# Two experts of a mixture share the weight stream block by block

## The chip, the cores and the metric

The kernel runs on one core of one Trainium2 chip. The metric is the device time of one execution in microseconds. All matrix products are made in fp32 split in two: a weight w is turned into a rounded part (fp32r) and a remainder, and products are formed from the parts.

## What is computed

Two transformer layers over 256 tokens of width 1024. Each has a mixer (retention, latent attention and an mLSTM side by side), a layer norm, a feed-forward part and a second layer norm. The feed-forward part of layer 0 is dense, that of layer 1 is a mixture of eight experts. Only this last part is touched:

```python
logits = (t @ router).astype(jnp.float32)
top_v, top_i = lax.top_k(logits, 2)
top_w = jax.nn.softmax(top_v, axis=-1)
gate = jnp.sum(jax.nn.one_hot(top_i, 8) * top_w[..., None], axis=1)
for e in range(8):
    y = y + gate[:, e:e + 1] * ((silu(t @ wg[e]) * (t @ wu[e])) @ wd[e])
```

The matrices wg[e] and wu[e] are 1024x3584 and wd[e] is 3584x1024. With 256 tokens and two experts for each token, an expert gets 64 tokens on average. In these inputs experts 0, 1, 3 and 6 get at most 64 tokens, and experts 2, 4, 5 and 7 get more.

## The kernel before

The experts are worked in pairs, in the order `ORDER = [(0, 1), (2, 3), (4, 5), (6, 7)]`, and within a pair one expert is finished before the other begins. An expert has seven blocks of 512 hidden columns. `UNITS` lists the 56 blocks in their order. In a block TensorE makes three products from six weight pieces of 1 MB (128x2048 fp32): "gate" (two pieces, `half_mm`), "up" (two pieces, `half_mm`) and "down" (two pieces, `down`). The down product belongs to the block before: its hidden values must first be activated, multiplied, transposed and split. So a block's order on TensorE is gate of this block, up of this block, down of the previous block.

Each piece passes through four engines. SyncE issues its load into a "raw" place. ScalarE copies it as fp32r (the high part, L356) and VectorE subtracts that from the original (the low part, L357); both parts go to a pair of split places (`next_whole`). TensorE then uses the pair and so frees it. There are three pairs of split places and eleven raw places (four of `ring`, five of "e1r", two of "eb", taken in turn by `WHERE`), and three places more that are used once at the start. ScalarE and VectorE work in program order. `feed.conv` says how many half pieces ahead of TensorE's use a split is written into that order: with 4, the split of the second next piece is placed when a piece is begun.

TensorE has two ways of making a product, and a branch on the expert's token count chooses (`products`). With more than 64 tokens it makes three passes, high by high, low by high and high by low (L387 to L389), so 12 matmuls of 512 columns for a piece. With at most 64 tokens, the high parts of the tokens fill one half of the array and the low parts the other, so that two passes do (L1579, 8 matmuls for a piece), and the upper half of the result is added to the lower by one more matmul (L1603, `fold_in`), for which ScalarE copies the upper half out (L1600, `lower`). I call the two kinds three-pass and two-pass blocks.

`turn` transposes a block's hidden values (L1627 in three-pass blocks, L1633 in two-pass blocks, where there are eight small transposes in place of four) and splits them (ScalarE L397, VectorE L398, tile hT); down needs both. Where the next block belongs to the same expert, the transposes are put into the branch of the first quarter of up. Otherwise they have a branch of their own ahead of up. Likewise the fold of up's result stands inside a branch of down where the neighbour is of the same expert. Otherwise `folded` makes a branch of its own, and its three-pass side holds a small matmul of 8 columns (L1611) that only closes the accumulation. `hidden` is the Silu on ScalarE (L1615) and `hidden_times` the product of gate and up on VectorE (L1618).

The rest of the work hangs between the blocks as tasks, and `little()` advances the first of them by one step: `gather` (one-hot matmuls that collect the tokens of the next pair's experts, L1509, L1514, L1515, eight steps), `scatter` (scaling of a finished expert's sum, L1683 and L1684, and the matmuls that bring a pair's results back to the tokens, L1690 and L1715) and `way_back` (L1531 to L1537). Before the first counts are known (`fullest`), blocks run three passes without a branch. An expert's sum `z` takes two of the eight PSUM banks for as long as the expert runs; gate, up, the transposes and the tasks take the others in turn.

The loop body that the change edits:

```python
pg, low_g = half_mm(e)
little()
...
pu, low_u = half_mm(e, {0: split_hidden, 1: lambda: lower(pg, low_g)},
                    first, {3: [lambda: fold_in(pg, low_g)]} if low_g is not None else {})
little()
```

In `half_mm` and `down`, the dictionaries say what is written into the program after which of a product's four quarters.

Of the kernel before, what the change touches and what calls it, by code (L numbers as in the profile page):

```python
# [32 lines left out]
PIECE = 2048  # L33
NRING = 4
T1, T2, M2 = 6, 5, 2
# [25 lines left out]
FDN = 7  # L61
WHERE = [None] * 4 + ["e1r"] * 5 + ["eb"] * NEB
ONCE = ["xg0", "xg1", "xp"]
XG = ["xg%d" % i for i in (0, 1, 2, 3, 0, 1, 2, 3)]
CAP = 128
# [4 lines left out]
NS = D_FE // 512  # L70
ORDER = [(0, 1), (2, 3), (4, 5), (6, 7)]
UNITS = [(e, s) for pair in ORDER for e in pair for s in range(NS)]
LATS = [{
# [198 lines left out]
def tile_hybrid_block(  # L272
# [13 lines left out]

    ring = enter(name="ring", bufs=NRING)
    whl = enter(name="whl", bufs=MHL)
# [24 lines left out]
    def piece(src, a, b, by_col=False, pair=None, raw=None, cut=None, fine=False, at_once=False):  # L313


        if raw == "big":
            w = big([PIECE], F32)
        else:
            pl, n = raw or (ring, NRING)
            tag, n = (n, 1) if isinstance(n, str) else ("w", n)  # L320
            w = pl.tile([P, PIECE], F32, tag=tag, bufs=n, name="w")
        wv = w[:, :a * b].rearrange("p (a b) -> p a b", a=a)
# [42 lines left out]
    pairs = list(range(MHL))  # L365

    def next_whole():

        two = pairs[:2]
        pairs[:] = pairs[2:] + two  # L370
        return [whl.tile([P, PIECE], F32R, tag="wp%d" % i, bufs=1, name="wp") for i in two]

# [145 lines left out]
    def mixer(l, mq, ml, tabs, then):  # L518
# [77 lines left out]
        if l == 0:  # L596

            xv2 = x_t.rearrange("(k p) n -> p k n", p=P)
            xr = ring.tile([P, PIECE], F32, tag="w", name="xr").rearrange("p (k n) -> p k n", k=KT)
# [655 lines left out]
    def moe_weights():  # L1255
# [10 lines left out]
        def add(src, a, b):  # L1266
# [6 lines left out]
            else:  # L1273
                feed.add(lambda: piece(src, a, b, at_once=True, fine=fine))

# [8 lines left out]
        def quarters(w):  # L1284

            t = ring.tile([P, PIECE], F32, tag="w", bufs=NRING, name="w")
            tv = t.rearrange("p (k h n) -> p k h n", k=2, h=2)
# [135 lines left out]
    def moe(mp, free_order):  # L1423
# [159 lines left out]

        def half_mm(e, after={}, first=((), ()), few={}):
            xg = state[e][0]
            ps = bank()
            for k in range(0, KT, 2):
                if k % 4 == 0:
                    pcs = feed.next()
                m = pcs[k % 4 // 2]  # L1590
                products(e, [(ps, xg[:, k + i], [q[:, i] for q in m], k + i == 0, k + i == KT - 1) for i in range(2)],
                         first if k == 0 else ((), ()), few.get(k // 2, ()))
                soon_one()
# [26 lines left out]
        def turn(e, s, joined=False):  # L1620
# [19 lines left out]
            if last:  # L1640
                hT = mp.tile([P, 4, 2, P], F32R, tag=XG[5], name="hl")
            else:
# [106 lines left out]
        inner.enter_context(tc.manual_schedule(engines={mybir.EngineType.Activation, mybir.EngineType.DVE}))  # L1749
        feed.conv = 4  # L1750
        for i_, (e, s) in [(i // (2 * NS), u) for i, u in enumerate(UNITS)]:
            if s == 0:
                soon_all()
            end = (e, s) == UNITS[-1]
            pg, low_g = half_mm(e)
            little()
            split_hidden, first = lambda: None, ((), ())
            if prev and prev[0] == e and e in many:
                split_hidden, first = turn(*prev, True)
            elif prev:  # L1760
                split_hidden = turn(*prev)
            pu, low_u = half_mm(e, {0: split_hidden, 1: lambda: lower(pg, low_g)},
                                first, {3: [lambda: fold_in(pg, low_g)]} if low_g is not None else {})
            little()
            if prev:
                same = prev[0] == e and low_u is not None and not end

                def product():
                    if not same:
                        folded(e, pu, low_u)  # L1770
                    hidden(e, s, pg)
                    if end:
                        hidden_times(e, s, pu)

                down(*prev, {0: lambda: lower(pu, low_u), 1 if end else 2: product,
                             3: (lambda: turn(e, s)()) if end else lambda: hidden_times(e, s, pu)},
                     {2: [lambda: fold_in(pu, low_u)]} if same else {})
# [5 lines left out]
            else:  # L1783
                lower(pu, low_u)
                folded(e, pu, low_u)
                hidden(e, s, pg)
                hidden_times(e, s, pu)
            if s == 3 and e == ORDER[i_][0] and i_ + 1 < len(ORDER):
                tasks.append(gather(ORDER[i_ + 1]))
# [19 lines left out]
        with tc.If(v > CAP):  # L1809
            for e in range(NE):  # L1810
# [16 lines left out]
                with tc.For_i(0, D_FE, P) as f0:  # L1827
                    wg_ = ring.tile([P, PIECE], F32, tag="w", name="wgx")
                    wu_ = ring.tile([P, PIECE], F32, tag="w", name="wux")
                    wd_ = ring.tile([P, PIECE], F32, tag="w", name="wdx")  # L1830
                    wgv = wg_[:, :D].rearrange("p (k f) -> p k f", k=KT)
# [126 lines left out]
```

## Time and profile before

| what | value |
|---|---|
| time, median of three runs | 1393.18 us (1392.72 to 1393.56) |
| time of the profiled execution | 1393.02 us |
| span of the profiled execution | 1391.2 us |
| granted TensorE clock, mean | 0.994 of full speed |
| TensorE matmul busy | 1344.7 us, 97% |
| VectorE busy | 1195.2 us, 86% |
| ScalarE busy | 1004.8 us, 72% |
| first Silu of the experts | at 474.51 us |
| 56th and last Silu of the experts | at 1361.89 us |

The busy shares are averages over stages with different limits, so the table does not say what sets the pace of the experts. A matmul's end is modelled in this profile, so that a busy TensorE can still lose time: what it loses is read from the weight loads, which follow each other at an even pace when nothing is waited for.

### The profile page before, as it was taken

The numbers are of one execution on the slowest core, as the hardware profiler recorded it, in microseconds if no ns is written. First come the engines' busy times: TensorE is split into PE (matmuls) and PEld (weight loads), VectorE is DVE, ScalarE is ACT, GpSimd is POOL, SyncE is SP. The second block draws the span as 40 slices with busy tenths as digits, with TensorE's granted clock in tenths as the row PEclk, the third lists the DMA queues.
The fourth block names the chain that finished last, engine by engine and source line by source line (L and its number), as shares of the span: only waits on it lengthen the run. The fifth ranks groups of instructions, "written<-read, shape, count | busy, mean of one in ns | idle before, by whom it ended". The sixth has DMA issues, their size and how long they took to land. (4 is left out here: it accounts for less than half of the span.)

```text
span 1391.2 us, 19646 instructions
## 1 busy us (share of the span) xinstructions
PE 1344.7 (97%) x7021; PEld 1094.9 (79%) x7021; DVE 1195.2 (86%) x1358; ACT 1004.8 (72%) x1057; POOL 41.8 (3%) x66
## 2 busy tenths in 40 slices
PE   9999999999999999999999999999999999999995
PEld 8887999998888867666788866688888887667884
DVE  7998735468878899999988899988889889999895
ACT  6743534435733699999877899878788888988883
POOL 1021000001021000000000000000000000000000
PEclk9999999999999999999999999999999999999998
DMA  9373835663147989999999999999999999999961
GB/s 346 118 238 130 274 121 182 212 210 123 60 184 298 334 321 405 403 401 406 406 395 364 359 383 403 405 406 395 352 366 362 383 377 361 405 402 404 405 242 51
DMA packets 200036, 431.11 MB, mean 310 GB/s; under 512 B 9824, under 2 KB 44000, under 8 KB 199904
## 3 DMA queue, kind: packets, MB, share of 16 engines
q1 hardware_dynamic: 195952, 425.01, 82.4%
q0 software_dynamic: 864, 3.15, 0.6%
q8 instruction: 92, 1.51, 0.4%
q10 hardware_dynamic: 3088, 1.11, 0.4%
q14 instruction: 40, 0.33, 0.1%
HBM read 428.19 MB, written 1.05 MB: 309 GB/s over the span
## 5 line engine op out<-in xcount | busy, mean ns | idle before, releaser
L357 DVE TENSOR_TENSOR wp<-w,wp 128x2048 fp32r<-128x2048 f32 (+3 forms) x382 | 734.6, 1944 | 116.4 <-ACT wp L356 113.6
L356 ACT CAST wp<-w 128x2048 fp32r<-128x2048 f32 (+3 forms) x382 | 618.4, 1632 | 170.8 <-PE pm L389 48.3
L1579 PE MATMUL pm<-wp,xg 128*128 128x512 f32 x848 | 218.5, 404 | 3.8 <-DVE wp L357 1.7
L1579 PEld LDWEIGHTS pm<-wp,xg 128*128 128x128 f32 x848 | 153.0, 189 | 55.2 <-DVE wp L357 23.1
L387 PE MATMUL pm<-wp,xg 128*128 128x512 f32 x472 | 186.8, 396 | 0.0
L388 PE MATMUL pm<-wp,xg 128*128 128x512 f32 x472 | 184.4, 391 | 0.6 <-DVE wp L357 0.5
L389 PE MATMUL pm<-wp,xg 128*128 128x512 f32 x472 | 184.2, 390 | 0.0
L357 DVE TENSOR_TENSOR wp<-big,wp 128x2048 fp32r<-128x2048 f32 (+1 forms) x66 | 136.9, 2093 | 9.9 <-ACT wp L356 9.1
L1579 PE MATMUL z<-wp,hT 128*128 128x512 f32 x448 | 117.2, 403 | 17.8 <-DVE hT L398 15.6
L356 ACT CAST wp<-big 128x2048 fp32r<-128x2048 f32 (+1 forms) x66 | 115.0, 1757 | 13.7 <-PE pm L389 10.0
L1579 PEld LDWEIGHTS z<-wp,hT 128*128 128x128 f32 x448 | 80.0, 188 | 44.7 <-issue 25.9
L388 PEld LDWEIGHTS pm<-wp,xg 128*128 128x128 f32 x472 | 88.7, 188 | 19.6 <-DVE wp L357 2.2
L389 PEld LDWEIGHTS pm<-wp,xg 128*128 128x128 f32 x472 | 88.6, 188 | 18.8
L387 PEld LDWEIGHTS pm<-wp,xg 128*128 128x128 f32 x472 | 88.7, 188 | 17.8
L392 PE MATMUL pm<-big,wp 128*128 128x256 f32 x320 | 90.6, 283 | 0.0
L394 PE MATMUL pm<-big,wp 128*128 128x256 f32 x320 | 90.6, 283 | 0.0
L393 PE MATMUL pm<-big,wp 128*128 128x256 f32 x320 | 90.5, 283 | 0.0
L387 PE MATMUL z<-wp,hT 128*128 128x512 f32 x216 | 85.0, 393 | 0.0
L389 PE MATMUL z<-wp,hT 128*128 128x512 f32 x216 | 84.3, 390 | 0.2
L388 PE MATMUL z<-wp,hT 128*128 128x512 f32 x216 | 84.2, 390 | 0.0
L531 PE MATMUL pm<-wp,big 128*128 128x512 f32 (+1 forms) x288 | 69.5, 389 | 0.6 <-ACT big L397 0.2
L1600 ACT CAST low<-pm 64x512 fp32r<-64x512 f32 x109 | 63.5, 583 | 2.7
(325 smaller groups left out, 1818.5 us busy)
## 6 DMA issues: line engine op xcount, KB each, us to landing
w<-in_moe_w_up_dram SPq DMA_DIRECT2D x93, 1024.0 KB, 9.1
w<-in_moe_w_gate_dram SPq DMA_DIRECT2D x89, 1024.0 KB, 8.1
w<-in_moe_w_down_dram SPq DMA_DIRECT2D x88, 1024.0 KB, 8.8
big<-in_moe_w_gate_dram SPq DMA_DIRECT2D x21, 1024.0 KB, 10.1
big<-in_moe_w_down_dram SPq DMA_DIRECT2D x20, 1024.0 KB, 7.7
big<-in_moe_w_up_dram SPq DMA_DIRECT2D x17, 1024.0 KB, 8.0
w<-in_w_in_dram SPq DMA_DIRECT2D x16, 1024.0 KB, 7.7
w<-in_ffn_w_gate_dram SPq DMA_DIRECT2D x11, 1024.0 KB, 5.8
```

Source lines behind the costliest of these rows:

```text
L356: act.copy(hv[c], src_[c])
L357: dve.tensor_tensor(lv[c], src_[c], hv[c].bitcast(F32), op=OP.subtract)
L387: pe.matmul(ps, s[0], m[0], start=first, stop=False)
L388: pe.matmul(ps, s[0], m[1], start=False, stop=False)
L389: pe.matmul(ps, s[1], m[0], start=False, stop=last)
L392: pe.matmul(ps, s[0], m[0], start=first, stop=False)
L393: pe.matmul(ps, s[1], m[0], start=False, stop=False)
L394: pe.matmul(ps, s[0], m[1], start=False, stop=last)
L531: pe.matmul(o, s, m, start=start, stop=stop)
L1579: pe.matmul(ps, both, m[part], start=begin and part == 0, stop=last and part == 1)
L1600: act.copy(low[0][HALF:], ps[HALF:])
```

## The change

`ORDER` pairs expert 0 with 4, 1 with 5, 2 with 6 and 3 with 7, and `UNITS` runs the pair's blocks alternately: block 0 of expert 0, block 0 of expert 4, block 1 of expert 0, and so on. Every pair then has one two-pass and one three-pass expert. As two experts are open at a time, their sums hold four PSUM banks.

Two of the four `ring` places stay raw places, and when the experts' pieces begin the other two become a fourth pair of split places. Raw places are then nine (`MRING, 2`), and twelve pieces instead of fourteen can be loaded in advance. `feed.conv` goes from 4 to 5, so that the split of the third next piece is placed in the middle of a piece.

The transposes of the previous block's hidden values now stand ahead of the last quarter of gate, and their split behind gate. As two blocks in a row are never of one expert, they always have a branch of their own, and the fold of up's result is always made by `folded`, with L1611 on the three-pass side. The copy `lower` of up's result moves from behind down's first quarter to behind its second, and `hidden_times` from behind down's fourth quarter to behind its third. The first block is followed by one more `little()`, so that the token counts are loaded ahead of the second block. The tags of the gathered tokens (`XG`) follow the new pairs.

```diff
-NRING = 4
+NRING, MRING = 4, 2
...
-WHERE = [None] * 4 + ["e1r"] * 5 + ["eb"] * NEB
+WHERE = [None] * MRING + ["e1r"] * 5 + ["eb"] * NEB
...
-XG = ["xg%d" % i for i in (0, 1, 2, 3, 0, 1, 2, 3)]
+XG = ["xg%d" % i for i in (0, 2, 0, 2, 1, 3, 1, 3)]
...
-ORDER = [(0, 1), (2, 3), (4, 5), (6, 7)]
-UNITS = [(e, s) for pair in ORDER for e in pair for s in range(NS)]
+ORDER = [(0, 4), (1, 5), (2, 6), (3, 7)]
+UNITS = [(e, s) for pair in ORDER for s in range(NS) for e in pair]
...
+    wholes = []
+
     def next_whole():
-
-        two = pairs[:2]
-        pairs[:] = pairs[2:] + two
-        return [whl.tile([P, PIECE], F32R, tag="wp%d" % i, bufs=1, name="wp") for i in two]
+        if not wholes:
+            wholes[:] = [[(whl, "wp%d" % i) for i in pairs[j:j + 2]] for j in range(0, MHL, 2)] + [[(ring, n) for n in routes["free"]]]
+        wholes.append(wholes.pop(0))
+        return [pl.tile([P, PIECE], F32R, tag=n, bufs=1, name="wp") for pl, n in wholes[-1]]
...
-        feed.conv = 4
+        feed.conv = 5
...
-            pg, low_g = half_mm(e)
+            turned, first, before = [], {}, {}
+            if prev and prev[0] == e:
+                split, first[3] = turn(*prev, True)
+                turned.append(split)
+            elif prev:
+                before[3] = lambda: turned.append(turn(*prev))
+            pg, low_g = half_mm(e, {3: lambda: turned[0]() if turned else None}, first, {}, before)
             little()
-            split_hidden, first = lambda: None, ((), ())
-            if prev and prev[0] == e and e in many:
-                split_hidden, first = turn(*prev, True)
-            elif prev:
-                split_hidden = turn(*prev)
-            pu, low_u = half_mm(e, {0: split_hidden, 1: lambda: lower(pg, low_g)},
-                                first, {3: [lambda: fold_in(pg, low_g)]} if low_g is not None else {})
+            pu, low_u = half_mm(e, {1: lambda: lower(pg, low_g)}, {},
+                                {3: [lambda: fold_in(pg, low_g)]} if low_g is not None else {})
...
-                    if end:
-                        hidden_times(e, s, pu)
-
-                down(*prev, {0: lambda: lower(pu, low_u), 1 if end else 2: product,
-                             3: (lambda: turn(e, s)()) if end else lambda: hidden_times(e, s, pu)},
+                    hidden_times(e, s, pu)
+
+                down(*prev, {0 if end else 1: lambda: lower(pu, low_u), 1 if end else 2: product,
+                             3: (lambda: turn(e, s)()) if end else lambda: None},
                      {2: [lambda: fold_in(pu, low_u)]} if same else {})
...
                 hidden_times(e, s, pu)
+                little()
```

## Rows read from the trace of the kernel before

**Rows 1.** Windows: busy time of each engine in stretches of experts 2, 3, 5, 6

```profile
core 0: us, PE busy (x) PEld busy (x) DVE busy (x) ACT busy (x) POOL busy (x), PEclk, DMA share, GB/s
...
686.00:796.00 110.00, 110.00 (x519) 91.90 (x518) 96.50 (x67) 86.21 (x73) 0.00 (x0) 1.00 1.02 376
...
811.00:898.00 87.00, 80.93 (x351) 56.45 (x350) 86.96 (x51) 81.65 (x63) 0.00 (x0) 1.00 1.04 400
...
1025.00:1142.00 117.00, 117.00 (x530) 96.62 (x529) 104.26 (x59) 96.12 (x73) 0.00 (x0) 1.00 1.01 375
...
1156.00:1247.00 91.00, 86.75 (x382) 62.00 (x381) 90.70 (x57) 82.77 (x66) 0.00 (x0) 1.00 1.03 391
```

**Rows 2.** Timeline of a two-pass block of expert 1: start, duration, engine, [idle before]

```profile
615.29 0.30 PEld L1579 LDWEIGHTS pm<-wp,xg 128*128 128x128 f32 x2
...
620.96 2.98 PE L1579 MATMUL z<-wp,hT 128*128 128x512 f32 x12 [0.86 <-DVE hT L398]
...
629.71 0.30 PEld L1579 LDWEIGHTS pm<-wp,xg 128*128 128x128 f32 x2
```

**Rows 3.** Timeline, weight loads of two three-pass blocks at the edge of experts 4, 5

```profile
1028.39 0.19 PEld L389 LDWEIGHTS pm<-wp,xg 128*128 128x128 f32 x1
...
1029.29 0.19 PEld L388 LDWEIGHTS pm<-wp,xg 128*128 128x128 f32 x1
...
1038.39 0.19 PEld L389 LDWEIGHTS z<-wp,hT 128*128 128x128 f32 x1
1038.93 0.13 PEld L1611 LDWEIGHTS pm<-fold 64*64 64x64 f32 x1 [0.35 <-issue]
...
1039.19 0.19 PEld L388 LDWEIGHTS z<-wp,hT 128*128 128x128 f32 x1
...
1045.56 0.19 PEld L389 LDWEIGHTS pm<-wp,xg 128*128 128x128 f32 x1
...
1046.45 0.19 PEld L388 LDWEIGHTS pm<-wp,xg 128*128 128x128 f32 x1
```

**Rows 4.** Waits of TensorE (PE, PEld) from 474 to 1362 us: total, times, longest

```profile
PE z L1579 <- DVE hT L398: 15.6, 18, 0.9
...
PEld pm L1579 <- DVE wp L357: 23.1, 57, 1.6
...
PEld pm L388 <- DVE wp L357: 2.2, 4, 0.8
```

**Rows 5.** First and last Silu of the experts (56 in all), ScalarE's timeline

```profile
474.51 0.60 ACT L1615 ACTIVATE sgm<-pm 128x512 f32<-128x512 f32 x1
...
1361.89 0.60 ACT L1615 ACTIVATE sgm<-pm 128x512 f32<-128x512 f32 x1
```

**Rows 6.** Timeline, gate's first weight load at both ends of two mixed blocks

```profile
795.01 1.09 PEld L1579 LDWEIGHTS pm<-wp,xg 128*128 128x128 f32 x5
...
810.40 1.11 PEld L1579 LDWEIGHTS pm<-wp,xg 128*128 128x128 f32 x5
...
1246.33 0.19 PEld L387 LDWEIGHTS pm<-wp,xg 128*128 128x128 f32 x1
...
1262.18 0.19 PEld L387 LDWEIGHTS pm<-wp,xg 128*128 128x128 f32 x1
```

**Rows 7.** VectorE and ScalarE groups by line and shape, 474 to 1362 us: busy, mean ns

```profile
L357 DVE TENSOR_TENSOR wp<-w,wp 128x2048 fp32r<-128x2048 f32 x265 | 600.2, 2287 | 45.5 <-ACT wp L356 42.9 <-DMA w<-in_moe_w_up_dram 0.9 <-DMA big<-in_moe_w_gate_dram 0.4
L356 ACT CAST wp<-w 128x2048 fp32r<-128x2048 f32 x264 | 501.4, 1910 | 73.0 <-PE pm L389 43.7 <-PE z L389 11.1 <-PE pm L1603 7.5
...
L1618 DVE TENSOR_TENSOR sgm<-sgm,pm 128x512 f32<-128x512 f32 x55 | 37.4, 680 | 0.0
```

**Rows 8.** Loads issued, KB each and median us to landing: 960:1025, then 640:686

```profile
w<-in_moe_w_up_dram SPq DMA_DIRECT2D x4, 1024.0 KB, 7.0
...
w<-in_moe_w_up_dram SPq DMA_DIRECT2D x5, 1024.0 KB, 14.0
```

**Rows 9.** VectorE's timeline: the token counts of all experts are ready

```profile
475.88 0.16 DVE L1474 CAST counts<-cnt 1x8 int32<-1x8 f32 x1
```

More of the change, by code (lines that the diff above doesn't have):

```diff
@@ L285, in gap, with ring_tile @@
         pl.tile([P, n // 4], F32, tag=tag, bufs=1, name=tag)
-    ring = enter(name="ring", bufs=NRING)
+    ring = enter(name="ring", bufs=1)
+    ring_turn = ["w%d" % i for i in range(NRING)]
+    def ring_tile(name="w"):
+        ring_turn.append(ring_turn.pop(0))
+        return ring.tile([P, PIECE], F32, tag=ring_turn[-1], name=name)
     whl = enter(name="whl", bufs=MHL)
@@ L318, in piece @@
         else:
-            pl, n = raw or (ring, NRING)
-            tag, n = (n, 1) if isinstance(n, str) else ("w", n)
-            w = pl.tile([P, PIECE], F32, tag=tag, bufs=n, name="w")
+            if raw is None:
+                w = ring_tile()
+            else:
+                pl, n = raw
+                tag, n = (n, 1) if isinstance(n, str) else ("w", n)
+                w = pl.tile([P, PIECE], F32, tag=tag, bufs=n, name="w")
         wv = w[:, :a * b].rearrange("p (a b) -> p a b", a=a)
@@ L598, in mixer @@
             xv2 = x_t.rearrange("(k p) n -> p k n", p=P)
-            xr = ring.tile([P, PIECE], F32, tag="w", name="xr").rearrange("p (k n) -> p k n", k=KT)
+            xr = ring_tile("xr").rearrange("p (k n) -> p k n", k=KT)
             for j in range(4):
@@ L1273, in add, with common @@
             else:
-                feed.add(lambda: piece(src, a, b, at_once=True, fine=fine))
+                def common():
+                    if len(ring_turn) > MRING:
+                        routes["free"] = ring_turn[MRING:]
+                        del ring_turn[MRING:]
+                    return piece(src, a, b, at_once=True, fine=fine)
+                feed.add(common)
         def whole(w, s_):
@@ L1284, in quarters @@
         def quarters(w):
-            t = ring.tile([P, PIECE], F32, tag="w", bufs=NRING, name="w")
+            t = ring_tile()
             tv = t.rearrange("p (k h n) -> p k h n", k=2, h=2)
@@ L1582, in products, with half_mm @@
                     f()
-        def half_mm(e, after={}, first=((), ()), few={}):
+        def half_mm(e, after={}, first={}, few={}, before={}):
             xg = state[e][0]
@@ L1590, in half_mm @@
                 m = pcs[k % 4 // 2]
+                before.get(k // 2, lambda: None)()
                 products(e, [(ps, xg[:, k + i], [q[:, i] for q in m], k + i == 0, k + i == KT - 1) for i in range(2)],
-                         first if k == 0 else ((), ()), few.get(k // 2, ()))
+                         first.get(k // 2, ((), ())), few.get(k // 2, ()))
                 soon_one()
@@ L1640, in turn @@
             if last:
-                hT = mp.tile([P, 4, 2, P], F32R, tag=XG[5], name="hl")
+                hT = mp.tile([P, 4, 2, P], F32R, tag="xg1", name="hl")
             else:
@@ L1827, in moe @@
                 with tc.For_i(0, D_FE, P) as f0:
-                    wg_ = ring.tile([P, PIECE], F32, tag="w", name="wgx")
-                    wu_ = ring.tile([P, PIECE], F32, tag="w", name="wux")
-                    wd_ = ring.tile([P, PIECE], F32, tag="w", name="wdx")
+                    wg_ = ring.tile([P, PIECE], F32, tag="w0", name="wgx")
+                    wu_ = ring.tile([P, PIECE], F32, tag="w1", name="wux")
+                    wd_ = ring.tile([P, PIECE], F32, tag="w2", name="wdx")
                     wgv = wg_[:, :D].rearrange("p (k f) -> p k f", k=KT)
```

## The prediction

> **What bounds the kernel now.** I read the windows first, expert by expert, to see which engine is full in which stretch. The reader should see two regimes [rows 1]. In the three-pass experts (2 and 5 are shown; 4 and 7 are of the same kind) TensorE is busy in all of the stretch, 110.00 of 110 us and 117.00 of 117, while VectorE has a tenth free (96.50 and 104.26). In the two-pass experts (3 and 6 are shown, 0 and 1 are of their kind) it is the other way: VectorE is busy 86.96 of 87 us and 90.70 of 91, and TensorE is not (80.93 and 86.75). The loads run at 400 and 391 GB/s beside the two-pass experts and at 376 and 375 beside the three-pass ones, where the places are full and the queue has to wait. So three engines take turns as the bound, and the experts stand one behind the other, so that what one regime leaves free can't serve the other.
>
> Then the timeline, for the length of a block. A two-pass block runs from 615.29 to 629.71, 14.42 us [rows 2], and this is VectorE's own work: six splits and two operations of 512 columns. Single ones take 2.287 and 0.680 us [rows 7], which overlap at their ends. TensorE waits in each such block, for instance 0.86 us for the low part of hT [rows 2]. A three-pass block is measured between the second loads behind two sets of transposes, 1029.29 and 1046.45, which is 17.16 us, L1611 included [rows 3]. L1611 costs this: from the load at 1029.29 to that at 1038.39 there are 40 steps, 0.2275 us each; the second load behind L1611 stands at 1039.19, which is 0.80 after 1038.39 where two steps would be 0.455. So L1611 costs 0.34 us, and a three-pass block inside an expert 16.82.
>
> The list of waits says what TensorE loses in all of the experts' phase [rows 4]: 15.6 us for hT, and 23.1 and 2.2 us of its weight loads for splits, 40.9 together. 61 of these gaps hold the 0.04 us that stand between any two loads (0.2275 less 0.19), 2.4 us, so 38.5 are real. The phase, first to last Silu, takes 887.4 us [rows 5]. Blocks account for 27 x 14.42 + 28 x 16.82 = 860.3 of it; the other 27.1 are gathers, scatters and the ways back.
>
> **The change part by part.** Alternation: a pair of blocks costs 14.42 + 16.82 = 31.24 us now. Its TensorE work is 14.42 less the waits of a two-pass block (38.5 over 28 blocks, 1.4 us), 13.0, plus 16.82, so 29.9. VectorE's work is at most 28.84 for the pair, as it is full in a two-pass block. If the lead of the splits evens out the two kinds, TensorE sets the pace of both, and the 38.5 us go: **-38.5**. The down product moves to the neighbour, which helps: a two-pass block now holds the down of a three-pass one, 8 matmuls more, 1.8 us, and gives its eight small transposes away; it should take about 14.4, and a three-pass block about 15.8 with L1611. The kernel before has one such block of each kind in its trace, where experts meet: 15.85 us for the three-pass kind (1246.33 to 1262.18) and 15.39 for the two-pass kind (795.01 to 810.40) [rows 6]. The first agrees. The second still has about 1.0 us of waits in it, and this is the argument's weak spot.
>
> L1611: it stands in each of 28 three-pass blocks, where it stood five times. 23 x 0.34 = **+7.8**. It waits for ScalarE's copy of up's result, a quarter later than before; ScalarE then has six copies of 1.91 us and four short ones, under 14 us in blocks of 14.4 and 15.8, so I add nothing. If that cover goes, the matmuls of down's second half queue behind it.
>
> Own branches for transposes: those of the first block of expert 5 have one (just behind 1028.39), those of its second block have not (just behind 1045.56). From the last load ahead to the second behind, the first takes 1029.29 - 1028.39 = 0.90 us and the second 1046.45 - 1045.56 = 0.89 [rows 3]. So 0: the branch is hidden behind matmuls already queued. The Trainium skill (Advanced Engine Details and Errata, Control Flow Timing) puts a compare-and-branch at about 108 ns; at two more in each of 56 blocks that would be 12 us and a time of 1384, if they were exposed. The trace doesn't agree that they are.
>
> Counts loaded ahead of the second block: they are ready at 476.04 (475.88 + 0.16) [rows 9], while the second block's gate now begins close to the first Silu, 474.51 [rows 5]. TensorE waits 1.5 us and the time of a register load; bounds 0 and 5, since the splits go on meanwhile. I take **+2.5**.
>
> Transposes in gate's last quarter: hT's split gets all of up as cover, 16 or 24 matmuls, 3.6 to 5.5 us. Ahead of it on VectorE stand up to two splits, 4.6 us. So in a two-pass block hT can still come late by a few tenths. `hidden_times` a quarter earlier puts the next splits behind a wait for up's fold; they need their free place anyhow. Four split places and `conv` 5 let VectorE run up to three pieces ahead; a two-pass block takes nothing from this lead (14.42 against 14.4), and a three-pass block adds 15.8 - 14.42.
>
> What is left of the waits can't be read from this trace. Bounds: 0, and all 38.5, as now; the mixed block of [rows 6], with 1.0 us, lies at 28 for 28 blocks. But that block ran with two pieces of lead, late transposes and a VectorE that came out of a scatter, so I go near the lower end, 0.25 per pair of blocks: **+7**. In gathers, ScalarE waits in order for TensorE's gather matmuls; this is in that number. The 27.1 us of tasks stay.
>
> Raw places, nine for eleven: 12 pieces lie ready, 324 remain. At 400 GB/s one takes 2.62 us, together 849 us, against 866 for the phase in my sum. So loads are covered, closely. With eleven places, time to landing grew from 7.0 us where the queue was held back to 14.0 at the end of two two-pass experts [rows 8]. Those blocks drew 6.29 MB in 14.42 us, 436 GB/s; alternating ones draw 12.58 MB in 30.2 us, 417, so the places drain half as fast.
>
> The sum: -38.5 + 7.8 + 2.5 + 7 = -21.2. From the profiled execution's 1393.0 us (1391.2 of span and 1.8 around it; the median of the runs is 1393.2), **1372 us**.
>
> **The rivals.** First, on the other side: VectorE and ScalarE keep setting the pace of two-pass blocks. Each block works in a fixed order, and VectorE's hT and sgm operations wait for TensorE in between. If the lead is lost there each time, the two-pass blocks keep their waits, 38.5 us in place of my 7, and the costs come on top: 1372 - 7 + 38.5 = 1403. It decides where what is left passes 28 us, that is 1.0 us per pair. For it speaks the mixed block, which lies at this point; against it VectorE's 1.4 us of room in each three-pass block, which follows each two-pass one. Chance 0.22, spread over faster (0.08), same (0.07) and slower (0.07).
>
> Second: loads become the bound. A pair of blocks needs 12.58 MB, 31.5 us at 400 GB/s, more than TensorE's 30.2. If nine places could store nothing of what is loaded during the tasks, the difference, 28 x 1.3 = 36 us, would come on top of all else: 1408. But landing times show that eleven places bridge at least 14.0 - 7.0 = 7 us, and seven pairs need 9; so I take a quarter of the 36, which is 1381. Landing times that reached 14 us speak for it. Chance 0.08. The Trainium skill (SBUF — State Buffer, A bandwidth-pool intuition that's wrong (but worth ruling out)) gives about 358 GB/s between HBM and a core and says that HBM is almost always the bottleneck. By it 352 MB take 984 us, and no reordering could gain. The 887.4 us that the phase took, and 400 GB/s in a row, disagree, and the measurement decides.
>
> Third: PSUM. Four banks are left for gate, up, transposes and tasks. If up gets the bank that the transposes have just left, it waits for hT's split behind two others, 4.6 us in each block, over 200 us: far slower. Rotation among the free banks makes it unlikely; short waits in gathers are the milder form. Chance 0.06 with that, slower. For the change not doing what it says I keep 0.02, slower.
>
> **How the numbers follow.** My forecast has 0.62, with a range of its own from 1361 (nothing left of the waits and no start cost give 1362) to 1384. Faster by over 0.2% (2.8 us, about what the runs shown can tell from no change): 0.62 + 0.08 + 0.08 = 0.78. Within: 0.07. Slower: 0.07 + 0.06 + 0.02 = 0.15. The range of 1360 to 1394 leaves out the slower cases and little below.
>
> **What would show it.** Right: Silus of a pair of blocks 30.2 to 30.5 us apart; TensorE's waits for hT and for splits down from 40.9 us to under 10; L1611 28 times at 0.34 us; loads near 400 GB/s without the dips to 375; landing times between 8 and 14 us and no large wait for them. Wrong: pairs at 31 us or more with VectorE full and TensorE waiting (first rival), ScalarE or VectorE waiting for loads (second), TensorE waiting for readers of a bank (third).

## The result, and the profile after

The changed kernel takes 1377.45 us (median of four runs, 1376.32 to 1377.93) where the kernel before takes 1392.95 beside it (1392.56 to 1393.56): a ratio of 0.9891, 95% interval 0.9878 to 0.9904. The profiled execution took 1377.93 us with a span of 1376.2, 15.0 less than before.

Lines have moved: the split is now L365 (ScalarE) and L366 (VectorE), the passes L398 to L400 and L1597, hT's split L408 and L409, `lower` L1619, the fold L1622, the closing matmul L1630, the Silu L1634, `hidden_times` L1637 and the small transposes L1652.

First the windows, two stretches of alternating blocks, with the columns of [rows 1], and the page's row of what the DMA engines moved in each of 40 slices:

```profile
560.00:590.00 30.00, 29.87 (x139) 23.33 (x137) 28.89 (x21) 25.89 (x22) 0.00 (x0) 1.00 1.04 406
...
1170.00:1230.00 60.00, 59.98 (x274) 46.82 (x273) 56.99 (x35) 51.92 (x42) 0.00 (x0) 1.00 1.04 402
```

```profile
GB/s 346 116 229 150 276 123 184 215 182 121 93 109 320 291 204 407 405 409 389 403 398 368 398 405 397 399 403 376 387 406 399 390 404 405 401 406 405 405 374 33
```

The two regimes of [rows 1] are gone. TensorE is busy in 59.98 of 60 us, VectorE in 56.99. From the 16th slice to the 38th, loads stay near 400 GB/s, with short dips, the lowest to 368.

Then the timeline of the weight loads, the first one of gate in two successive blocks, and the Silus of three more:

```profile
1197.83 2.69 PEld L1597 LDWEIGHTS pm<-wp,xg 128*128 128x128 f32 x12
...
1212.25 0.19 PEld L398 LDWEIGHTS pm<-wp,xg 128*128 128x128 f32 x1
...
1228.10 2.70 PEld L1597 LDWEIGHTS pm<-wp,xg 128*128 128x128 f32 x12
```

```profile
475.09 0.60 ACT L1634 ACTIVATE sgm<-pm 128x512 f32<-128x512 f32 x1
497.80 0.60 ACT L1634 ACTIVATE sgm<-pm 128x512 f32<-128x512 f32 x1
...
1209.99 0.60 ACT L1634 ACTIVATE sgm<-pm 128x512 f32<-128x512 f32 x1
1227.01 0.60 ACT L1634 ACTIVATE sgm<-pm 128x512 f32<-128x512 f32 x1
1240.27 0.60 ACT L1634 ACTIVATE sgm<-pm 128x512 f32<-128x512 f32 x1
...
1347.37 0.60 ACT L1634 ACTIVATE sgm<-pm 128x512 f32<-128x512 f32 x1
```

From gate to gate a two-pass block takes 14.42 us (1197.83 to 1212.25) and a three-pass block 15.85 (to 1228.10), which answers to [rows 2, 3]: 14.42 and 17.16 there. A block's Silu stands behind its up, inside the down product of its neighbour, so that Silus divide the same pair differently: they stand 17.02 (to that of a three-pass block) and 13.26 us (to that of a two-pass block) apart, 30.28 together, 31.24 before. The phase from first to last Silu [rows 5] is 872.3 us, 15.1 less than the 887.4 of before. The first interval is the exception: 22.71 us.

The waits of TensorE in this phase, which answer to [rows 4]: total, times, longest.

```profile
PE pm L1549 <- issue: 4.2, 1, 4.2
...
PE z L1597 <- DVE hT L409: 0.9, 1, 0.9
PE pm L1597 <- DVE wp L366: 0.4, 1, 0.4
```

```profile
PEld pm L1630 <- ACT low L1619: 9.5, 24, 0.6
...
PEld pm L1597 <- DVE wp L366: 1.3, 2, 0.8
```

What was 15.6 us for hT is 0.9, and what was 23.1 and 2.2 us for splits is 1.3 of weight loads (and 0.4 of matmuls). The largest of what is left are gaps of at most 0.6 us each ahead of the folds and the closing matmuls, which the groups by line show below, gaps of 0.35 us ahead of the small transposes, and one wait of 4.2 us at the start. That start, on VectorE, TensorE and ScalarE ([rows 9] shows the same counts before):

```profile
476.96 0.16 DVE L1492 CAST counts<-cnt 1x8 int32<-1x8 f32 x1
```

```profile
474.43 0.17 PE L1488 MATMUL pm<-ck,mxr 16*1 16x16 f32 x1
478.76 0.68 PE L1549 MATMUL pm<-ck,oh 128*128 128x128 f32 x2 [4.16 <-issue]
...
479.95 0.77 PE L398 MATMUL pm<-wp,xg 128*128 128x512 f32 x1
480.53 0.63 PE L399 MATMUL pm<-wp,xg 128*128 128x512 f32 x1
...
485.22 0.46 PE L398 MATMUL pm<-wp,xg 128*128 128x512 f32 x1
```

```profile
480.00:500.00 20.00, 20.00 (x84) 15.81 (x85) 12.79 (x9) 14.18 (x13) 0.00 (x0) 0.87 0.46 165
```

The counts are ready at 477.12, 2.5 us after TensorE's last matmul, and TensorE goes on at 478.76, 1.64 us later. From 480.53 to 485.22 there are 11 steps, 0.426 us each, where 0.2275 is the pace elsewhere. 512 columns in 0.427 us are 1.2 GHz, the lower of the clock's two levels; the window from 480 has a mean granted clock of 0.87.

Durations by line and shape, answering to [rows 7], and loads to landing for the windows of [rows 8]:

```profile
L366 DVE TENSOR_TENSOR wp<-w,wp 128x2048 fp32r<-128x2048 f32 x251 | 566.7, 2287 | 30.9 <-ACT wp L365 26.3
L365 ACT CAST wp<-w 128x2048 fp32r<-128x2048 f32 x249 | 470.8, 1909 | 58.1 <-PE pm L400 46.5 <-PE z L400 8.4 <-PE z L1597 1.9
...
L1622 PEld LDWEIGHTS pm<-low,fold 64*64 64x64 f32 x54 | 7.0, 129 | 19.3 <-issue 7.8 <-ACT low L1619 6.6 <-ACT sgm L1634 4.9
...
L1630 PEld LDWEIGHTS pm<-fold 64*64 64x64 f32 x28 | 3.6, 129 | 10.9 <-ACT low L1619 9.5 <-issue 1.4
```

```profile
w<-in_moe_w_up_dram SPq DMA_DIRECT2D x6, 1024.0 KB, 8.3
...
w<-in_moe_w_up_dram SPq DMA_DIRECT2D x5, 1024.0 KB, 8.5
```

A split or a copy takes as long as before. Landings, 7.0 and 14.0 us before, are 8.3 and 8.5, which fits places that are freed at an even pace.

### The profile page after: what moved, and what is told of

Read it like the earlier page. It is cut to its first block, busy times and chain, and to the rows that moved or that the text cites. A ratio compares the mean times of both kernels' runs of the same rounds, so it can differ in the third digit from the quotient of the medians.

```text
span 1376.2 us, 19796 instructions
## 1 busy us (share of the span) xinstructions
PE 1342.7 (98%) x7037; PEld 1098.4 (80%) x7037; DVE 1193.2 (87%) x1358; ACT 998.4 (73%) x1058; POOL 41.8 (3%) x66
## 5 line engine op out<-in xcount | busy, mean ns | idle before, releaser
L366 DVE TENSOR_TENSOR wp<-w,wp 128x2048 fp32r<-128x2048 f32 (+3 forms) x372 | 703.1, 1917 | 95.6 <-ACT wp L365 91.1
L365 ACT CAST wp<-w 128x2048 fp32r<-128x2048 f32 (+3 forms) x372 | 591.4, 1610 | 159.3 <-PE pm L400 48.4
L1597 PE MATMUL pm<-wp,xg 128*128 128x512 f32 x864 | 210.5, 394 | 1.5 <-PE z L1597 1.1
L1597 PEld LDWEIGHTS pm<-wp,xg 128*128 128x128 f32 x864 | 159.2, 188 | 35.3 <-PE z L1597 2.0
L398 PE MATMUL pm<-wp,xg 128*128 128x512 f32 x464 | 185.7, 400 | 0.0
L399 PE MATMUL pm<-wp,xg 128*128 128x512 f32 x464 | 182.0, 392 | 0.0
L400 PE MATMUL pm<-wp,xg 128*128 128x512 f32 x464 | 181.9, 392 | 0.0
L366 DVE TENSOR_TENSOR wp<-big,wp 128x2048 fp32r<-128x2048 f32 (+1 forms) x76 | 165.3, 2203 | 11.5 <-ACT wp L365 11.3
L365 ACT CAST wp<-big 128x2048 fp32r<-128x2048 f32 (+1 forms) x76 | 138.5, 1845 | 22.9 <-PE pm L400 19.0
L1597 PE MATMUL z<-wp,hT 128*128 128x512 f32 x448 | 114.5, 398 | 1.4 <-DVE hT L409 0.9
L398 PEld LDWEIGHTS pm<-wp,xg 128*128 128x128 f32 x464 | 87.8, 189 | 19.5
L400 PEld LDWEIGHTS pm<-wp,xg 128*128 128x128 f32 x464 | 87.7, 189 | 19.2
L1597 PEld LDWEIGHTS z<-wp,hT 128*128 128x128 f32 x448 | 81.5, 188 | 19.4 <-ACT wp L365 1.1
L398 PE MATMUL z<-wp,hT 128*128 128x512 f32 x216 | 90.1, 417 | 0.0
L400 PE MATMUL z<-wp,hT 128*128 128x512 f32 x216 | 84.3, 390 | 0.0
L1619 ACT CAST low<-pm 64x512 fp32r<-64x512 f32 x110 | 64.1, 582 | 3.1 <-PE pm L400 0.5
```

Of the source, the lines that this page charges most:

```text
L365: act.copy(hv[c], src_[c])
L366: dve.tensor_tensor(lv[c], src_[c], hv[c].bitcast(F32), op=OP.subtract)
L398: pe.matmul(ps, s[0], m[0], start=first, stop=False)
L399: pe.matmul(ps, s[0], m[1], start=False, stop=False)
L400: pe.matmul(ps, s[1], m[0], start=False, stop=last)
L1597: pe.matmul(ps, both, m[part], start=begin and part == 0, stop=last and part == 1)
```

## The experiments

All but the last two start from the changed kernel (1377.45 us); those two start from the first.

**Counts loaded later.** The counts are loaded behind the second block's gate, as before the change. The transposes of the first block's hidden values, whose branch needs the counts, follow there, ahead of up.

```diff
+            early = prev and e not in many
...
-            elif prev:
+            elif prev and not early:
...
+            if early:
+                turned.append(turn(*prev))
-            pu, low_u = half_mm(e, {1: lambda: lower(pg, low_g)}, {},
+            pu, low_u = half_mm(e, {0: lambda: turned[0]() if early else None, 1: lambda: lower(pg, low_g)}, {},
...
                 hidden_times(e, s, pu)
-                little()
```

> The changed kernel, but the token counts are loaded behind the second block's gate, as in the kernel before, and that one block's transposes follow behind gate. Theory (the start costs what its rows show: 4.2 us of TensorE's wait for the counts and some 3 us of matmuls at the lower clock behind it): 7 us faster than the changed kernel, 1370 to 1371. Rival (the splits are behind anyhow, so the wait only changes its name): 1375 to 1377.

1370.77 us (1370.42 to 1371.15), ratio to before 0.9842 (0.9826 to 0.9859). The first two Silus:

```profile
475.24 0.60 ACT L1634 ACTIVATE sgm<-pm 128x512 f32<-128x512 f32 x1
490.72 0.60 ACT L1634 ACTIVATE sgm<-pm 128x512 f32<-128x512 f32 x1
```

The first interval is 15.48 us in place of 22.71, 7.23 less, and the time fell by 6.7. The early load of the counts cost that much.

**TensorE kept busy in that wait.** 75 small matmuls on constants stand ahead of the load of the counts.

```diff
                 hidden_times(e, s, pu)
+                warm(75)
                 little()
```

> The changed kernel with 75 small bf16 matmuls of no use ahead of the load of the counts, so that TensorE is busy in the wait; the wait for the counts stays. Theory (the clock falls because TensorE stands idle for 4.2 us): the clock stays up, 12 matmuls of 512 columns at 0.23 in place of 0.43 us and some transposes, about 3 us faster than the changed kernel, 1374 to 1375. Rival (the lower clock hides behind splits that are late in any case): 1377 to 1378.

1375.95 us (1375.17 to 1376.85), 0.9879 (0.9862 to 0.9895). In TensorE's timeline:

```profile
475.62 4.36 PE L416 MATMUL pm<-ck 128*128 128x128 bf16 x75
480.50 0.43 PE L1549 MATMUL pm<-ck,oh 128*128 128x128 f32 x2 [0.52 <-PE pm L416]
...
481.69 0.39 PE L400 MATMUL pm<-wp,xg 128*128 128x512 f32 x1
481.91 0.40 PE L398 MATMUL pm<-wp,xg 128*128 128x512 f32 x1
```

The matmuls behind the wait now keep the pace of 0.23 us, and the first interval is 20.29 us, 2.42 less. That is the price of the lower clock, and it agrees with the steps: from 479.95 to 485.22 the changed kernel has 12 steps, 5.27 us where 2.73 would do. In time it gave 1.5 us, between theory and rival: 1.08 us were lost again ahead of the first Silu, which stands at 476.17 here, before the added matmuls begin. No run says why; in the kernels of this study the first Silu stands anywhere from 471.2 to 476.2. So the 7.2 us are 4.2 of wait, about 2.5 of clock, and 0.5 that I can't place.

**Like experts in a pair.** Two-pass experts alternate with two-pass ones, three-pass with three-pass.

```diff
-XG = ["xg%d" % i for i in (0, 2, 0, 2, 1, 3, 1, 3)]
+XG = ["xg%d" % i for i in (0, 1, 2, 0, 3, 2, 1, 3)]
-ORDER = [(0, 4), (1, 5), (2, 6), (3, 7)]
+ORDER = [(0, 1), (2, 4), (3, 6), (5, 7)]
```

> The changed kernel, but experts of one kind are paired: 0 with 1, 2 with 4, 3 with 6, 5 with 7. Blocks still alternate between experts and all other parts stay. Theory (the gain is that a block that is short of VectorE stands beside one that is short of TensorE): two-pass blocks back at 14.4 us, three-pass blocks 16.8 plus 0.34 for L1611's successor, so no gain and the costs on top, 1400 to 1408. Rival (the places and the earlier transposes gain by themselves): 1375 to 1382.

1403.87 us (1402.19 to 1404.11), 1.0077 (1.006 to 1.0094): slower than before. Three-pass Silus stand 17.16 to 17.18 us apart, two-pass ones 14.4 in the steady part, and TensorE waits for hT again:

```profile
PE z L1597 <- DVE hT L409: 10.3, 12, 0.9
```

These are the blocks of before, with L1630 in each three-pass one, and the two regimes are back: VectorE is busy in all of the 30 us from 560, among two-pass blocks, and TensorE in all of the 30 us from 1170, among three-pass ones. Alternation without the mix of kinds gains nothing.

**One expert after the other.** All other parts of the change stay, but as neighbouring blocks are of one expert again, transposes and folds go back into the neighbour's branches.

```diff
-UNITS = [(e, s) for pair in ORDER for s in range(NS) for e in pair]
+UNITS = [(e, s) for pair in ORDER for e in pair for s in range(NS)]
```

> The changed kernel, but a pair's experts run one after the other, as before the change; four split places, nine raw ones and transposes in gate's last quarter stay. Transposes and the fold are then joined to neighbouring branches again. Theory (alternation is the gain): two-pass blocks at 14.4, three-pass blocks at 16.8 us, 1390 to 1398 with the start's cost. Rival (places and earlier transposes gain): two-pass blocks under 13.6 us, 1370 to 1378.

1385.72 us (1385.62 to 1386.2), 0.9952 (0.9935 to 0.9968): neither. Alternation, with the closing matmuls and branches that it brings, is worth 8.3 us, and the other parts 6.7, after the start's cost is paid. Silus inside the two-pass expert 6 show how: they stand 13.26, 13.88, 14.40, 14.44 and 14.40 us apart. The lead that a three-pass expert left is used up within a few blocks, and VectorE's own 14.4 us are back.

**Three places.** Three split places, eleven raw ones, and the shorter lead (`feed.conv`), with alternation.

```diff
-NRING, MRING = 4, 2
+NRING, MRING = 4, 4
...
-            wholes[:] = [[(whl, "wp%d" % i) for i in pairs[j:j + 2]] for j in range(0, MHL, 2)] + [[(ring, n) for n in routes["free"]]]
+            wholes[:] = [[(whl, "wp%d" % i) for i in pairs[j:j + 2]] for j in range(0, MHL, 2)]
...
-        feed.conv = 5
+        feed.conv = 4
```

> Alternation and the earlier transposes, but with the places of the kernel before: three pairs of split places, eleven raw ones, and the split of the second next piece placed in the order (4 half pieces ahead). Theory (the fourth place carries VectorE's lead over a two-pass block): waits of TensorE for splits come back, 0.3 to 0.5 us per block, 1390 to 1400. Rival (alternation alone is enough): 1376 to 1380.

1428.49 us (1428.07 to 1430.04), 1.0261 (1.0244 to 1.0278): far beyond the theory's upper end. Pairs take 32.6 us, and TensorE's waits for splits are larger than before the change:

```profile
PEld pm L1597 <- DVE wp L366: 42.9, 89, 1.6
...
PEld z L399 <- DVE wp L366: 14.5, 23, 0.7
```

**Four places, the shorter lead.** Only the last line of that diff.

```diff
-        feed.conv = 5
+        feed.conv = 4
```

> The changed kernel with one number put back: feed.conv is 4 and not 5, so that a split is written into the order of ScalarE and VectorE two pieces ahead and not two and a half; the four split places and nine raw places stay. The run with three places and the shorter lead lost 51 us against the changed kernel; this tells which of the two lost it. Theory: the fourth place did the work, and the lead has little to do with it: pairs of Silus stay within 0.2 us of 30.28, the time is 1375 to 1383. Rival: the lead did, because a split that comes late in the order stands behind hT's split: pairs of 31.5 us or more, 1410 to 1430.

1390.95 us (1388.99 to 1392.05), 0.9988 (0.9979 to 0.9998): between the two. The place is worth 37.5 us (1428.5 to 1391.0) and the lead 13.5 more; by the phase from first to last Silu alone (924.3, 889.0 and 872.3 us) 35.4 and 16.7. Pairs take 30.65 us, with these waits:

```profile
PEld z L399 <- DVE wp L366: 12.8, 23, 0.7
...
PEld pm L1597 <- DVE wp L366: 10.8, 23, 1.1
```

**One expert after the other with three places.** The edits of two runs above together, "One expert after the other" and "Three places" (the diff shows its first and its last line).

```diff
-UNITS = [(e, s) for pair in ORDER for s in range(NS) for e in pair]
+UNITS = [(e, s) for pair in ORDER for e in pair for s in range(NS)]
...
-        feed.conv = 5
+        feed.conv = 4
```

> The kernel with the pairs (0, 4), (1, 5), (2, 6), (3, 7) worked one expert after the other (1385.7 us), now also with three split places, eleven raw places and the shorter lead, as in the kernel before. What is left of the change is the new pairs, the earlier transposes with their own branches, and the counts loaded ahead of the second block. Theory: without alternation too the fourth place is what gained, so the two-pass blocks fall back to 14.4 us or more, and the start's 7 us are paid on top: 1395 to 1402. Rival: the order of experts gained (a two-pass expert always starts behind a three-pass one, with full places), so the time stays at 1383 to 1389.

1396.11 us (1394.43 to 1397.49), 1.0022 (1.0012 to 1.0032): the theory. Without alternation the fourth place and the lead give 10.4 us; with it, 51.0. The first interval, with the early counts in it, is 21.37 us here and 15.61 before the change. Without these 5.8 us the kernel would stand some 2 us under the kernel before; what of that the new order of experts gives, no run separates.

**Transposes ahead of up again.**

```diff
             elif prev:
-                before[3] = lambda: turned.append(turn(*prev))
+                pass
...
+            if prev and not turned:
+                turned.append(turn(*prev))
-            pu, low_u = half_mm(e, {1: lambda: lower(pg, low_g)}, {},
+            pu, low_u = half_mm(e, {0: lambda: turned[0]() if turned else None, 1: lambda: lower(pg, low_g)}, {},
```

> The changed kernel, but the transposes stand ahead of up, as before the change, and their split behind up's first quarter. Theory (hT needs all of up as cover): hT comes late in the blocks that begin with a two-pass up, up to 0.9 us in 28 blocks, 1385 to 1400. Rival (with four places hT is early enough in either case): 1376 to 1379.

1376.93 us (1376.71 to 1377.42), 0.9889 (0.9873 to 0.9906), pairs of 30.28 us: the rival. With the lead that four places give, hT comes in time from either place, so this part of the change is worth nothing.

**Eight raw places.**

```diff
-NEB = 2
+NEB = 1
```

> The changed kernel with eight raw places in place of nine. Theory (loads are covered): under 2 us slower, 1377 to 1379. Rival (loads run at the edge, so that each place counts): 5 to 15 us slower, 1382 to 1392, with waits of ScalarE for loads.

1377.43 us (1376.81 to 1379.01), 0.9893 (0.9876 to 0.9909): loads are covered with a place to spare.

**The closing matmul on all rows.** L1630 uses 128 rows of the array and not 64.

```diff
-                    pe.matmul(ps[:HALF, :8], fold[:HALF], fold[:HALF, :8], start=False, stop=True, skip_group_check=True)
+                    pe.matmul(ps[:HALF, :8], eye[0][:, :HALF], fold[:, :8], start=False, stop=True, skip_group_check=True)
```

> The changed kernel, but the small matmul that closes up's sum in three-pass blocks (the successor of L1611) uses all 128 rows of the array in place of 64; it adds zeros in either case. Theory (its 0.34 us is that the weight load waits until the array has run empty, because the tile changes): about 0.25 us less in 28 blocks, 7 us, 1370 to 1371. Rival (it waits for ScalarE's copy behind which it stands, or a VectorE that has no room takes the time): 1376 to 1378.

1376.2 us (1375.17 to 1376.29), 0.9881 (0.9864 to 0.9897), pairs of 30.28: the rival. Some 0.7 of the 1.25 us gained lies outside the experts, whose phase is 871.7 us in place of 872.3. In 24 of the 28 closes L1630 has the gap all the same, and it names ScalarE's copy, which ends 0.05 or 0.06 us ahead:

```profile
526.94 0.13 PEld L1630 LDWEIGHTS pm<-fold,eye 128*64 128x64 f32 x1 [0.31 <-ACT low L1619]
```

In the other four the copy had ended 0.8 to 2.1 us earlier, and there the theory holds. One of them in the changed kernel, then here:

```profile
720.70 0.13 PEld L1630 LDWEIGHTS pm<-fold 64*64 64x64 f32 x1 [0.35 <-issue]
```

```profile
719.25 0.14 PEld L1630 LDWEIGHTS pm<-fold,eye 128*64 128x64 f32 x1
```

The 16 loads of down and the close take 3.99 us there (717.66 to 721.65) and 3.75 here (716.53 to 720.28), where 16 steps alone are 3.64. So with the copy long done the close costs 0.35 us on 64 rows and 0.11 on 128. With a copy that has just ended it costs 0.42 on either (555.37 to 559.43 in the changed kernel, 554.25 to 558.31 here).

**Folds and close on all rows, and the copy a quarter earlier.** From the first experiment's kernel.

```diff
-                act.copy(low[0][HALF:], ps[HALF:])
+                act.copy(low[0], ps)
...
-            pe.matmul(ps[:HALF], fold[HALF:], low[0][HALF:], start=False, stop=True, skip_group_check=True)
+            pe.matmul(ps[:HALF], fold, low[0], start=False, stop=True, skip_group_check=True)
...
-                    pe.matmul(ps[:HALF, :8], fold[:HALF], fold[:HALF, :8], start=False, stop=True, skip_group_check=True)
+                    pe.matmul(ps[:HALF, :8], eye[0][:, :HALF], fold[:, :8], start=False, stop=True, skip_group_check=True)
...
-                down(*prev, {0 if end else 1: lambda: lower(pu, low_u), 1 if end else 2: product,
+                down(*prev, {0: lambda: lower(pu, low_u), 1 if end else 2: product,
```

> The kernel with the counts loaded behind the second block (1370.8 us), and three things about the folds: ScalarE copies up's result behind down's first quarter again and not behind its second, the copy and the folds use all 128 rows, and so does the small matmul that closes the accumulation on the three-pass side (L1630). The earlier run with the close alone on 128 rows gained nothing, but its close stood right behind ScalarE's copy. Theory: two things hold the same 0.31 to 0.35 us, the copy and the change of the tile's rows, and with both away three such gaps in each pair of blocks go: pairs of 29.3 to 29.8 us, 1345 to 1358, or 1360 to 1364 if loads (12.58 MB in each pair) take over. Rival: the gap stands ahead of any weight load of 64 columns behind a branch, whatever its rows and its data, so pairs stay at 30.2 to 30.3 us and the time at 1369 to 1372.

1359.11 us (1358.39 to 1360.34), 0.9761 (0.9744 to 0.9777), the fastest kernel of the study. In the groups by line and shape, the last column is idle time ahead of the loads:

```profile
L1622 PEld LDWEIGHTS pm<-low,fold 128*64 128x64 f32 x54 | 7.2, 134 | 2.9
L1630 PEld LDWEIGHTS pm<-fold,eye 128*64 128x64 f32 x28 | 3.8, 134 | 1.1
```

It was 19.3 us ahead of the folds and 10.9 ahead of the closes in the changed kernel (19.2 and 11.0 in the first experiment's), so 26.2 us of gaps went. The small transposes, still on 64 rows, keep theirs:

```profile
L1652 PEld LDWEIGHTS pm<-ck,sgm 64*128 64x128 f32 x224 | 16.1, 139 | 9.5 <-issue 9.2 <-DVE wp L366 0.4
```

Two-pass intervals fell from 13.27 to 12.74 us, but three-pass ones rose from 17.01 to 17.16, so a pair takes 29.90, just above the theory's 29.3 to 29.8, and 27 pairs at 0.38 us less are 10.3 of the 11.7 us. The waits say where much of the rest went:

```profile
PEld z L399 <- DVE wp L366: 9.1, 19, 0.5
PEld z L400 <- DVE hT L409: 7.9, 19, 0.4
```

These two, 17.0 us together, are waits for VectorE, which is busy 29.09 of 30 us in the window from 1200. Loads move 406 GB/s there, and no wait of any size for them is in the lists of ScalarE and VectorE. Three things were changed at once, so the 11.7 us are their worth together; no run has the earlier copy alone.

**No closing matmul.** From the first experiment's kernel, too.

```diff
                 with tc.If(many[e] <= HALF) as cmp:
                     fold_in(ps, low)
-                with cmp.Else():
-
-                    pe.matmul(ps[:HALF, :8], fold[:HALF], fold[:HALF, :8], start=False, stop=True, skip_group_check=True)
```

> The kernel with the counts loaded behind the second block (1370.8 us), without the matmul that closes the accumulation on the three-pass side (L1630): three-pass blocks have no instruction there, and only the two-pass side of the branch has its fold. Nothing else is different. Theory: each of 28 such matmuls costs TensorE 0.42 us, so 11.8 us go: pairs of 29.85 us, 1357 to 1361. Rival: VectorE (28.8 us a pair) or the loads (12.58 MB in 29.85 us are 421 GB/s, where 400 to 411 were seen) take over, and what TensorE gives up turns into waits for splits: pairs of 30.1 to 30.3 us, 1366 to 1371.

1376.52 us (1375.84 to 1377.21), 0.9884 (0.9868 to 0.9901): 5.7 us slower than with the matmul, against theory and rival. Three-pass intervals are 17.33 us, 0.32 more, and VectorE has room (28.58 of 30 us from 1200). The timeline of this kernel, then that of the kernel with the matmul, for the same place:

```profile
517.96 2.68 PEld L1597 LDWEIGHTS z<-wp,hT 128*128 128x128 f32 x12
...
520.32 0.58 ACT L1619 CAST low<-pm 64x512 fp32r<-64x512 f32 x1
...
521.53 0.76 PEld L1597 LDWEIGHTS z<-wp,hT 128*128 128x128 f32 x4 [0.89 <-issue]
522.33 1.81 PEld L1597 LDWEIGHTS pm<-wp,xg 128*128 128x128 f32 x8
```

```profile
518.03 2.68 PEld L1597 LDWEIGHTS z<-wp,hT 128*128 128x128 f32 x12
...
520.39 0.58 ACT L1619 CAST low<-pm 64x512 fp32r<-64x512 f32 x1
...
521.07 0.13 PEld L1630 LDWEIGHTS pm<-fold 64*64 64x64 f32 x1 [0.35 <-ACT low L1619]
521.29 0.76 PEld L1597 LDWEIGHTS z<-wp,hT 128*128 128x128 f32 x4
522.10 2.02 PEld L1597 LDWEIGHTS pm<-wp,xg 128*128 128x128 f32 x9
```

With the matmul, TensorE goes on 0.10 us after the end of ScalarE's copy (520.97); without it, 0.63 us after (520.90). From the group of 12 loads to the load behind the group of 4 there are 16 steps, 3.64 us at 0.2275; 4.37 passed without the matmul and 4.07 with it. So the branch with an empty side costs 0.73 us and the one with the matmul 0.43. TensorE's list of waits names its own sequencer at L1626, the line of the branch:

```profile
PE z L1597 <- PEq L1626: 13.1, 27, 0.6
```

That TensorE waits for the copy ahead of the branch when the side is empty, and pays for the branch behind it, fits these numbers; no run separates it from another cause.

What each part is worth, from runs that differ by it (the kernel before by its 19 runs beside the last experiments):

| step | time, us | difference |
|---|---|---|
| kernel before | 1392.6 | |
| new order, early counts, transposes, copy and branches (one after the other, three places) | 1396.1 | +3.5 |
| with the fourth place and the longer lead | 1385.7 | -10.4 |
| with alternation: the changed kernel | 1377.5 | -8.3 |
| with the counts loaded later | 1370.8 | -6.7 |
| with folds on all rows and the earlier copy | 1359.1 | -11.7 |

## Why the prediction was right, point by point

The time, 1377.45, lies in the forecast's own range (1361 to 1384), 5 us above its 1372. The steady blocks came out nearly as worked out, and two terms beside them, the counts and the tasks, were too small.

- **TensorE sets the pace of a pair.** Right, nearly to the hundredth: blocks of 14.42 and 15.85 us where I had 14.4 and 15.8, pairs of 30.28 where I expected 30.2 to 30.5. The like pairs show that it is the mix that does it, and the runs with three places and with the shorter lead that the fourth place and the longer lead both carry it.
- **What is left of the waits, +7.** There is nothing left: 14.42 + 16.82 less 1.4 of waits, and 0.43 for L1630, are 30.27, and the rows have 30.28. The bound at the lower end was the true one. The mixed block of [rows 6], which I kept as the weak spot, had three places and the short lead; the run with these had waits for splits in most blocks and pairs of 32.6 us.
- **L1611, +7.8.** The mechanism was right and the size was not: 0.43 us each, not 0.34. The 0.34 was read [rows 3] from the only one of the five closes of the kernel before whose copy had long ended (1.45 us earlier). The other four waited for the copy; this one stands in the mixed block of [rows 6]:

```profile
1261.15 0.13 PEld L1611 LDWEIGHTS pm<-fold 64*64 64x64 f32 x1 [0.35 <-ACT low L1600]
```

It begins 0.09 us behind the end of the copy, and down and close take 4.06 us (1258.12 to 1262.18) where 16 steps are 3.64, so it cost 0.42 us already. The size could have been read before, and the quarter by which the copy moved did not raise it above this. I saw no cost in moving the copy, but in the changed kernel 24 of 28 closes stand right behind it, and there the 128-row close could gain nothing.
- **Steady blocks together.** 27 pairs at 0.96 us are -25.9 us where the terms above gave -23.7.
- **Counts ahead of the second block, +2.5.** This is one of the two terms that failed. The first interval is 22.71 us, 5.9 more than a three-pass block of before, and loading the counts later gives back 7.2. I took 1.5 us and a register load; TensorE waited 2.5 us until the counts were ready and 1.64 more, and I left out that it then ran at 1.2 GHz for 12 matmuls (2.5 us).
- **Tasks, 0.** 872.3 less the first interval (22.7) and 27 pairs (817.6) leaves 32.0 us beside the blocks, 27.1 before: +4.9. I had them stay, but for waits in gathers, which I put into the 7 us above. Most of it is in the gathers: the intervals of the three gathers exceed the steady ones by 14.9 us together, where they exceeded them by 10.9 before. Why they cost more beside alternating blocks, no run shows; that stays open.
- **The sum.** -25.9 + 5.9 + 4.9 = -15.1, which is what the phase lost; as the tasks are what is left over, it must come out. That the forecast came within 5 us owes something to luck: L1611, counts and tasks took some 12 us more than their terms, and the 7 us kept for waits, of which the steady blocks show none, made up for more than half of it.
- **Own branches for transposes, 0, and transposes in gate's last quarter.** The run with transposes ahead of up has the same pairs and the same time. Pairs that come out of matmul work alone leave no room for the 12 us that exposed branches would cost by the Trainium skill (Advanced Engine Details and Errata, Control Flow Timing). But a branch is not free everywhere: the one with an empty side cost 0.73 us.
- **Raw places.** Right: eight do as well as nine. The 358 GB/s of the Trainium skill (SBUF — State Buffer, A bandwidth-pool intuition that's wrong (but worth ruling out)) do not bind here: the windows show 402 and 406. The dips to 375 that I expected to go are still there in two of the 40 slices, at 368 and 376.
- **The rivals.** The first, VectorE and ScalarE keeping the pace, did not come. The kernel with three places has its waits for splits, but VectorE is not full there (55.02 of 60 us from 1200): what it lacks is the lead. The second, loads, and the third, PSUM, show no wait of any size in the lists.

## What to carry to other kernels

Where two kinds of work fill different engines, take them in turns, and give the lead of one engine over the other a place to stand in first: here alternation without the fourth place and the longer lead lost 36 us against the kernel before, and with them it gained 15, the start's cost included in both. Before costing a wait of TensorE at its length alone, look at the clock of the work behind it. When a gap has two causes of one length, taking one away can show nothing: test both together, and look for places where only one of them is at work.

## What the runs showed of the hardware

- **A load of 64 rows between loads of 128 rows has a gap of 0.35 us.** It came to 19.3 us ahead of 54 folds (64x64), and in the first experiment's kernel it was 0.35 whether their copy had ended 0.25 us or 3.5 us earlier. On 128 rows it went (2.9 us), although these tiles still have 64 columns, and the transposes of the same kernel, on 64 rows, kept it. The Trainium skill (TensorEngine Tiling (Array Packing), Key Properties) says that changing the tiling mode drains TensorE. The change of rows agrees; the change of columns alone (128x128 to 128x64) showed no such gap, and there the measurement decides.
- **Two causes can hide each other.** The closing matmul cost 0.42 us on 64 rows and on 128 rows where the copy had just ended. Where the copy was long done, it cost 0.35 on 64 rows, 0.11 on 128 rows, and in the kernel with all on 128 rows and the earlier copy 0.12 (518.47 to 522.23, 3.76 us against 3.64).
- **A branch with an empty side was dearer than one with a small matmul in it,** 0.73 us against 0.43, behind a copy that ends late in both.
- **A single wait of 4.2 us was followed by 12 matmuls at 0.427 us** in place of 0.2275, 2.5 us more; with other matmuls in the wait, the pace behind it was 0.23.
